# A hybrid attention and feed-forward layer on one core: ScalarE takes the forget logits, diagonal maxima in one masked pass, layer norm without a mean pass, and W1's first pieces on attention's tiles

## The chip, the cores and the metric

The kernel runs on one core of a Trainium2 chip. The metric is the device time of one execution in microseconds. TensorE (PE) does the matmuls and the transposes, VectorE (DVE), ScalarE (ACT) and GpSimd (POOL) the elementwise work, and SyncE (SP) and ScalarE's queue issue the transfers between HBM and the on-chip memory.

## The reference

One layer of a decoder, for a sequence of S = 2048 rows of width 1024, in float32:

```python
a = rms_norm(h, pre_mix_g)
z = a @ w_in                      # q | k | v (512 each) | forget logits (8) | u | v_sg (512 each)
y_att = forgetting_attention(q, k, v, f + f_bias)
y_sg = gelu(u) * (causal_mix(layer_norm(gelu(v_sg))) + bias)   # in chunks of 128 rows
y = concat(rms_norm(y_att), rms_norm(y_sg))
h = h + rms_norm(y @ w_out)
h = h + rms_norm(square(relu(rms_norm(h) @ w_ff1)) @ w_ff2)    # inner width 4096
h = h + sigmoid(h @ w_g + b_g) * (p @ w_pe)
```

Attention has 8 heads of 64. Its logits are q.k/8 + c[t] - c[s], where c is the running sum of log sigmoid(f + f_bias) over the rows, masked to s <= t. The layer norm takes a row's mean and its variance over 512 values, with a gain and an offset per column.

## The kernel before, in words

Every large matmul is done in three passes on operands split into a rounded part and the remainder (`mm3`, lines 102 to 106): high by high, high by low, low by high. The rounded parts are made by ScalarE or POOL, the remainders by VectorE or POOL (`split`, `halves_of`, `evac_split`).

**First stage (lines 221 to 523).** Four blocks of 512 rows. For each block, `block` runs six column groups of W_in, in the order v_sg's larger part (344 columns), the rest of u and v_sg (344), forget logits and u (344), q, k, v (512 each); each group has four output tiles n, and each output tile eight steps over the contraction. Step i = 4 x group + n names a place in this order, at which hooks hang other work: the layer norm from i = 8 on, `log_sigmoid` at 11, the running sum at 14, the spatial mix from 14 on, the next block's x at 11 to 22. Output tiles lie in two PSUM banks (`pacc`); the group's done function empties the bank. For the third group that is `fu_done` (lines 356 to 358): VectorE adds the bias to the 8 logits, then ScalarE applies gelu to the 336 columns of u in the same bank. For the second group it is `uv_done` (347 to 354): two gelus with row sums, the negative mean mu, `gv + mu` by VectorE (352), a Square with row sum by ScalarE. `layer_norm` (409 to 418) then takes the inverse deviation r and does (gv * r) * lng and + lnb on VectorE.

W_in's columns for the next group are loaded, rounded by ScalarE (line 96) and completed by POOL (line 100) in twelve tiles `wsp`, while the group before runs.

While block b is projected, a filler runs `maxima(b - 1)` (lines 142 to 189): the largest logit of each row over all keys, for each head, which attention's exponent needs. For a head and a key block c, four matmuls (one per 128 rows) write logits into the banks `pM` (two, and a third in this stage). VectorE reduces a bank to one column of `mx`. On the diagonal (c == b) it reduces the columns ahead of the last 128 and then handles the last 128 by a second operation that adds the triangular mask `dmask` and takes the maximum.

`log_sigmoid` (374 to 393) computes, for 512 rows and 8 heads held as 128 x 32, log sigmoid through a polynomial of eight terms, as a chain of small VectorE operations with one Sigmoid on ScalarE; `run_sum` (395) turns it into the running sum with two matmuls, one by the triangle `upper`, one by a tile of ones.

**Attention (528 to 930).** Heads and key blocks in an order written out by hand; the maxima of the last block and the projection by W_out of finished blocks run beside it.

**The passage (939 to 1256).** The projection of the last 512 rows (`last_proj`) runs with `prep_first` as filler, which normalises and transposes h for the feed-forward: `turn` goes through three tiles `px` and stores to `cS`, `join_now` makes the first two of four contraction steps of the operands B. The feed-forward's W1 product is done by seven products (a Strassen scheme) for each unit of 256 columns; `left` makes the sum of W1's blocks that a product needs, in two tiles `ws`, and splits it into one of three tiles `w1p`. The first unit runs in two halves: contraction steps 0 and 1 for all seven products, then 2 and 3, while `join` makes the operands of steps 2 and 3. `join` reads from `cS` into four tiles (`jraw`): the three px, and half of the tile w1raw[1]. `prep_next` does later what prep_first does, for the second half of the rows, with px as places too.

The order of instructions on each engine is set by the framework's scheduler, from the order in which the code traces them and from when it reckons them to be ready. Tiles live in pools that are stacked from two sides of the on-chip memory. A tile in a newly opened pool waits for the last use of those older tiles whose addresses it takes over. The three w1p lie in a pool of their own, `w1pp` (line 1134), opened after the projection's pools have been closed; its first tile takes over the addresses of the projection's last tiles, the two `z2` (lines 745 to 751 work on them).

Of the kernel before, what the change touches and what calls it, by code (L numbers as in the profile page):

```python
# [9 lines left out]
F32 = mybir.dt.float32  # L10
F32R = mybir.dt.float32r
AF = mybir.ActivationFunctionType
# [22 lines left out]
def trunk(ctx, tc, x, p, w_in, f_bias, sg_ln_g, sg_ln_b, sg_w, sg_b, att_out_g, sg_out_g,  # L35
# [4 lines left out]
    def pool(stack, name, bufs=1, space=None, side="left"):  # L40
# [30 lines left out]
    c_all = const1.tile([P, NT, H], F32, name="c_all")  # L71
    c0_all = const1.tile([P, NB, H], F32, name="c0_all")
    dmask_r = const1.tile([P, P], F32R, name="dmask")
# [4 lines left out]
    ident_r = const1.tile([P, P], F32R, name="ident_r")  # L78
    ve.tensor_copy(ident_r, ident)

# [58 lines left out]
    for t in QM:  # L139
        ve.memset(t[HD:HD + 2].bitcast(F32), 1.0)  # L140

    def maxima(b):

# [13 lines left out]
        for h in range(H):  # L157
            q = QM[h % 2]
            sc.dma_start(q[:HD].bitcast(F32), qS[b, h, :HD])
            mx = msm.tile([P, 4, 6], F32, name="mx")  # L160
            po.memset(mx, NEG)
            for c in range(b + 1):
                km = KM[n % NKM]
                n += 1
                sc.dma_start(km[:HD + 2].bitcast(F32), kS[c, h, HD:])
                for tt in range(4):
                    w = TB if c < b else P * (tt + 1)
                    ps = place_m()
                    pe.matmul(ps[:, :w], q[:, tt * P:(tt + 1) * P], km[:, :w], start=True, stop=True)  # L169
                    full = w if c < b else w - P  # L170
                    if full:
                        ve.tensor_reduce(mx[:, tt, c:c + 1], ps[:, :full], AX.X, ALU.max)  # L172
                    if c == b:
                        dg = ps[:, w - P:w]
                        ve.tensor_tensor_reduce(out=dg, in0=dg, in1=dmask, scale=1.0, scalar=NEG,
                                                op0=ALU.add, op1=ALU.max, accum_out=mx[:, tt, 5:6])
# [44 lines left out]
    with ExitStack() as ph:  # L221
# [19 lines left out]
        sgb = cst.tile([P, H], F32, name="sgb")  # L241
        ones = cst.tile([P, P], F32, name="ones")
        upper = cst.tile([P, P], F32, name="upper")
# [3 lines left out]
        def prep_consts():  # L247
            sy.dma_start(fb, f_bias[0].partition_broadcast(P))
            sy.dma_start(g_sgo, sg_out_g[0].rearrange("(k p) -> p k", p=P))
            sy.dma_start(lng, sg_ln_g[0].partition_broadcast(P))  # L250
            sy.dma_start(lnb, sg_ln_b[0].partition_broadcast(P))
            sy.dma_start(sgb, sg_b[0].rearrange("g t -> t g"))
            ve.memset(csum[:, 0], 0.0)
            ve.memset(ones, 1.0)
            po.affine_select(out=upper, in_=ones, pattern=[[1, P]], compare_op=ALU.is_ge, fill=0.0,
                             base=0, channel_multiplier=-1)
# [71 lines left out]
        def block(b, aT, hooks, fill, first=None):  # L328
# [18 lines left out]
            def uv_done(tt, ps):  # L347
# [3 lines left out]
                ve.tensor_scalar(mu[:, tt:tt + 1], mu[:, tt:tt + 1], -1.0 / AW, None, ALU.mult)  # L351
                ve.tensor_scalar(gv[:, tt], gv[:, tt], mu[:, tt:tt + 1], None, ALU.add)
                junk = sg1.tile([P, 512], F32, name="junk")
                sc.activation(junk, gv[:, tt], AF.Square, accum_out=ss[:, tt:tt + 1])

            def fu_done(tt, ps):
                ve.tensor_tensor(zf[:, tt], ps[:, :H], fb, ALU.add)
                sc.activation(ug[:, tt, :336], ps[:, H:344], AF.Gelu_apprx_tanh)  # L358
# [15 lines left out]
            def log_sigmoid():  # L374

                ve.tensor_scalar(e, zf, -1.0, None, ALU.mult)
                ve.tensor_tensor(e, zf, e, ALU.min)
                sc.activation(e, e, AF.Sigmoid)
# [3 lines left out]
                ve.tensor_tensor(s2, s_, s_, ALU.mult)  # L382
                ve.tensor_scalar(pl, s2, 1.0 / 17, 1.0 / 15, ALU.mult, ALU.add)
                for k in (13, 11, 9, 7, 5, 3, 1):
                    ve.tensor_tensor(pl, pl, s2, ALU.mult)
                    ve.tensor_scalar(pl, pl, 1.0 / k, None, ALU.add)
                ve.scalar_tensor_tensor(pl, pl, -2.0, s_, ALU.mult, ALU.mult)
                ve.tensor_scalar(zf, zf, 0.0, None, ALU.min)
                ve.tensor_tensor(pl, pl, zf, ALU.add)
                ve.tensor_copy(car[:, 0], csum[:, b])  # L390
# [4 lines left out]
            def run_sum():  # L395
                ps = pmx.tile([P, 512], F32, name="pmx")
                pe.matmul(ps[:, :32], upper, pl.rearrange("p a h -> p (a h)"), start=True, stop=False)
                pe.matmul(ps[:, :32], ones, car[:, 0:4].rearrange("p a h -> p (a h)"), start=False, stop=True)
                ve.tensor_copy(c_all[:, 4 * b:4 * b + 4].rearrange("p a h -> p (a h)"), ps[:, :32])
# [9 lines left out]
            def layer_norm():  # L409

                r = rstd_of(small, ss, 4, AW, "lnr")
                for tt in range(4):
                    ve.scalar_tensor_tensor(gv[:, tt], gv[:, tt], r[:, tt:tt + 1], lng, ALU.mult, ALU.mult)
                    ve.tensor_tensor(gv[:, tt], gv[:, tt], lnb, ALU.add)
                    po.tensor_scalar(vn[:, 0, tt], gv[:, tt], 1.0, 0.0, ALU.mult, ALU.add)
# [547 lines left out]
    ws = [fsm.tile([P, 4, P], F32, name=f"ws{e}") for e in range(2)]  # L963
    px = [w1q.tile([P, 4, P], F32, name=f"px{e}") for e in range(3)]

# [7 lines left out]

    _, w1raw = w1_places(w1q)


# [103 lines left out]

    flat = [t.rearrange("p a b -> p (a b)") for t in px]

# [14 lines left out]
    def prep_next():  # L1097

        for k in (3, 2, 1, 0):
# [6 lines left out]

            yield from join_now(k, 1, place, done, flat[0], flat[1], px[2], px[2])

    raws, nraw, nleft = {}, 2, 0
    lefts = {}  # L1110
# [22 lines left out]
    mix_stack.close()  # L1133
    w1p = w1_pieces(pool(w1s, "w1pp", side="right"))

# [227 lines left out]
    for i, (u, n, ks) in enumerate(run):  # L1363
        if i == len(JR):
# [3 lines left out]
            ctc = pool(fl, "ctc")  # L1368
            hqp = pool(fl, "hqp")
            for t in ((0, 0), (0, 1), (1, 0), (1, 1), 5, 6):  # L1370
                hq[t] = hqp.tile([P, 512], F32, name="hq" + str(t).strip("()").replace(", ", "_"))
# [250 lines left out]
```

## Time and profile before

| | |
|---|---|
| median of three runs | 2703.38 us (2702.57 to 2706.26) |
| the profiled execution | 2701.87 us, with a span of 2700.1 us |
| clock granted to PE, mean over the span | 0.989 |
| busy share of the span | PE 97%, PEld 79%, DVE 68%, ACT 50%, POOL 30% |
| HBM traffic | 174 GB/s over the span |

The span runs from the first instruction to the last; times in the views count from its start. Matmuls overlap, and their ends are modelled, so PE's idle time is read from the waits rather than from the starts. In a row of a timeline, the bracket at the end says how long the engine stood idle before the instruction and which instruction of which engine released it. Lines are those of the kernel before; L104 to L106 are the three passes of mm3, wherever it is called.

### The profile page before, as it was taken

How to read it: one execution, taken by the hardware profiler on the slowest of the kernel's cores; microseconds unless marked ns; L12 is line 12 of the kernel's file. 1: busy time of each engine (PE TensorE's matmuls, PEld its weight loads, DVE VectorE, ACT ScalarE, POOL GpSimd, SP SyncE). 2: the span in 40 equal slices, each digit the busy share in tenths (PEclk: the TensorE clock that was granted, in tenths of full speed). 3: DMA queues.
4: the chain of work that ended last, by engine and by line, in shares of the span. 5: the costliest groups of instructions: out<-in, count | busy, mean ns of one | idle time of the engine just before them, and what ended most of it. 6: DMA issues, size and time to landing. Idle time of an engine off the chain costs nothing.

```text
span 2700.1 us, 37436 instructions
## 1 busy us (share of the span) xinstructions
PE 2613.7 (97%) x12316; PEld 2123.4 (79%) x12316; DVE 1841.5 (68%) x3212; ACT 1342.4 (50%) x2632; POOL 811.5 (30%) x695
## 2 busy tenths in 40 slices
PE   8999999999899999969999999999999999999999
PEld 7787978777677777757788788888888888888887
DVE  5547576866778655578888676668886596875443
ACT  6444433358777777555555554544445444453111
POOL 5444343510000000253444332325451171501211
PEclk9999999999999999989999999999999999999999
DMA  5565756598868766454665854447556654673331
GB/s 169 151 183 145 195 141 171 145 218 211 210 177 190 175 182 151 137 164 165 224 210 175 296 193 148 150 155 247 171 191 223 187 160 132 210 250 115 109 119 61
DMA packets 440611, 472.85 MB, mean 175 GB/s; under 512 B 155616, under 2 KB 269664, under 8 KB 440416
## 3 DMA queue, kind: packets, MB, share of 16 engines
q1 hardware_dynamic: 430179, 454.39, 57.0%
q10 hardware_dynamic: 10237, 16.07, 2.2%
q8 instruction: 97, 1.59, 0.3%
q14 instruction: 98, 0.80, 0.1%
HBM read 336.38 MB, written 133.96 MB: 174 GB/s over the span
## 4 chain that ended last, share of the span: by engine, by line
PE 53%; DMA 2%; DVE 1%; issue 1%; ACT 1%; POOL 0%; SPq 0%; DVEq 0%; ACTq 0%; POOLq 0%
PE pf L106 17%; PE pf L104 17%; PE pf L105 17%; PE pf L1470 1%; DMA w1raw<-in_w_ff_dram 0%; DMA px<-hS 0%; DMA cS<-px 0%; DVE w1p L994 0%; DMA B<-jS 0%; PE pf L1018 0%; DVE ws L1170 0%; DVE hq L1189 0%; DVE z L748 0%; POOL tmp L1068 0%; DMA ysT<-ysS 0%
## 5 line engine op out<-in xcount | busy, mean ns | idle before, releaser
L104 PE MATMUL pf<-B,w1p 128*128 128x512 f32 x752 | 298.3, 397 | 14.4 <-ACT w1p L991 13.6
L106 PE MATMUL pf<-B,w1p 128*128 128x512 f32 x752 | 296.1, 394 | 2.8 <-DVE w1p L994 2.7
L1197 POOL TENSOR_TENSOR hq<-hq,hq 128x512 f32<-128x512 f32 x128 | 197.0, 1550 | 335.4 <-ACT hq L1191 298.3
L105 PE MATMUL pf<-B,w1p 128*128 128x512 f32 x752 | 297.1, 395 | 0.0
L660 DVE TENSOR_TENSOR hl<-pr,hl 128x512 fp32r<-128x512 f32 (+1 forms) x320 | 191.9, 608 | 102.7 <-ACT hl L659 86.0
L100 POOL TENSOR_TENSOR wsp<-wraw,wsp 128x344 fp32r<-128x344 f32 (+1 forms) x176 | 200.1, 1154 | 192.0 <-ACT wsp L96 181.6
L651 ACT ACTIVATE pr<-pS,bias 128x512 f32<-128x512 f32 (+1 forms) x320 | 196.6, 623 | 106.1 <-PE pS L647 64.0
L172 DVE TENSOR_REDUCE mx<-pM 128x1 f32<-128x512 f32 (+3 forms) x288 | 169.8, 597 | 78.7 <-PE pM L169 78.0
L104 PEld LDWEIGHTS pf<-B,w1p 128*128 128x128 f32 x752 | 141.7, 188 | 48.9 <-ACT w1p L991 14.1
L104 PE MATMUL pacc<-wsp,wide 128*128 128x344 f32 (+1 forms) x480 | 166.7, 347 | 9.7 <-ACT ug L358 6.8
L104 PE MATMUL pf<-R,L 128*128 128x512 f32 x452 | 175.9, 389 | 0.0
L106 PE MATMUL pf<-R,L 128*128 128x512 f32 x452 | 175.8, 389 | 0.0
L105 PE MATMUL pf<-R,L 128*128 128x512 f32 x452 | 175.8, 389 | 0.0
L106 PEld LDWEIGHTS pf<-B,w1p 128*128 128x128 f32 x752 | 141.5, 188 | 37.5 <-DVE w1p L994 4.4
L105 PEld LDWEIGHTS pf<-B,w1p 128*128 128x128 f32 x752 | 141.7, 188 | 31.9
L106 PE MATMUL pacc<-wsp,wide 128*128 128x344 f32 (+1 forms) x480 | 162.7, 339 | 0.5 <-DVE wide L117 0.5
L105 PE MATMUL pacc<-wsp,wide 128*128 128x344 f32 (+1 forms) x480 | 162.4, 338 | 0.0
L659 ACT CAST hl<-pr 128x512 fp32r<-128x512 f32 (+3 forms) x272 | 146.6, 549 | 6.5 <-PE pO L674 0.8
L991 ACT CAST L<-lr 128x512 fp32r<-128x512 f32 x113 | 70.3, 622 | 149.6 <-PE pf L105 119.5
L994 DVE TENSOR_TENSOR L<-lr,L 128x512 fp32r<-128x512 f32 x113 | 96.1, 851 | 68.0 <-ACT L L991 67.7
L994 DVE TENSOR_TENSOR w1p<-ws,w1p 128x512 fp32r<-128x512 f32 (+1 forms) x136 | 117.4, 869 | 35.7 <-ACT w1p L991 33.8
L991 ACT CAST w1p<-w1raw 128x512 fp32r<-128x512 f32 (+1 forms) x123 | 73.4, 598 | 128.5 <-PE pf L105 124.2
(443 smaller groups left out, 7199.1 us busy)
## 6 DMA issues: line engine op xcount, KB each, us to landing
hidC<-hq SPq DMA_DIRECT2D x224, 256.0 KB
lr<-hidC SPq DMA_DIRECT2D x224, 256.0 KB
w1raw<-in_w_ff_dram SPq DMA_DIRECT2D x64, 512.0 KB
w1raw<-in_w_ff_dram SPq DMA_DIRECT2D x128, 256.0 KB
wraw<-in_w_in_dram SPq DMA_DIRECT2D x96, 256.0 KB
wraw<-in_w_in_dram SPq DMA_DIRECT2D x88, 172.0 KB
KM<-kS ACTq DMA_DIRECT2D x80, 132.0 KB
jS<-C SPq DMA_DIRECT2D x19, 512.0 KB
```

The lines of the kernel that those rows point to most:

```text
L100: e.tensor_tensor(dst[:, 1], src, dst[:, 0].bitcast(F32), ALU.subtract)
L104: pe.matmul(ps, l[0], r[0], start=first, stop=False)
L105: pe.matmul(ps, l[0], r[1], start=False, stop=False)
L106: pe.matmul(ps, l[1], r[0], start=False, stop=last)
L172: ve.tensor_reduce(mx[:, tt, c:c + 1], ps[:, :full], AX.X, ALU.max)
L651: sc.activation(pr[:, off:], ps[:, off:], AF.Exp, bias=bias_of(b)[:, j, h:h + 1])
L659: sc.copy(hl[:, 0, off:], pr[:, off:])
L660: ve.tensor_tensor(hl[:, 1, off:], pr[:, off:], hl[:, 0, off:].bitcast(F32), ALU.subtract)
L991: sc.copy(dst[:, 0], src)
L994: (po if lo == "pool" else ve).tensor_tensor(dst[:, 1], src, dst[:, 0].bitcast(F32), ALU.subtract)
L1197: po.tensor_tensor(t, x, y, op)
L1470: pe.transpose(ps[:, kk], hts[t][g][:, kk * P:(kk + 1) * P], ident)
```

## The change

- **Forget logits.** In `fu_done` ScalarE copies the 8 logits out of the bank; the bias is added by VectorE once per block, at the head of `log_sigmoid`, on 128 x 32.
- **log_sigmoid.** The sum of negation and minimum becomes one operation, each Horner step becomes one (it was two), and the last steps are joined: 17 VectorE operations instead of 24.
- **Layer norm.** `gv + mu` goes; the Square takes mu as its bias; `layer_norm` becomes (gv + mu) * lng, then (.) * r + lnb.
- **Diagonal maxima.** One operation over all columns of the bank, with a mask `wmask` of 512 columns (384 zeros, then the triangle), its last w columns used; mx has four columns instead of six.
- **Small moves.** `ident_r` is made ahead of `dmask`; the tile of ones goes, and a broadcast column of `upper` stands for it.
- **W1's pieces.** The three w1p are allotted in w1q, the pool that is opened when attention's pools have been closed and before the projection of the last rows. To make room, px keeps one tile of its own and has the two ws as the others; jraw becomes both halves of w1raw[1], v_t and the last px; prep_next gets two tiles `pxn` from a later pool.

```diff
             for c in range(b + 1):
...
-                    full = w if c < b else w - P
-                    if full:
-                        ve.tensor_reduce(mx[:, tt, c:c + 1], ps[:, :full], AX.X, ALU.max)
-                    if c == b:
-                        dg = ps[:, w - P:w]
-                        ve.tensor_tensor_reduce(out=dg, in0=dg, in1=dmask, scale=1.0, scalar=NEG,
-                                                op0=ALU.add, op1=ALU.max, accum_out=mx[:, tt, 5:6])
+                    if c < b:
+                        ve.tensor_reduce(mx[:, tt, c:c + 1], ps, AX.X, ALU.max)
+                    else:
+                        ve.tensor_tensor_reduce(out=ps[:, :w], in0=ps[:, :w], in1=wmask[:, TB - w:], scale=1.0, scalar=NEG,
+                                                op0=ALU.add, op1=ALU.max, accum_out=mx[:, tt, c:c + 1])
...
-                ve.tensor_scalar(gv[:, tt], gv[:, tt], mu[:, tt:tt + 1], None, ALU.add)
                 junk = sg1.tile([P, 512], F32, name="junk")
-                sc.activation(junk, gv[:, tt], AF.Square, accum_out=ss[:, tt:tt + 1])
+                sc.activation(junk, gv[:, tt], AF.Square, bias=mu[:, tt:tt + 1], accum_out=ss[:, tt:tt + 1])
...
-                ve.tensor_tensor(zf[:, tt], ps[:, :H], fb, ALU.add)
+                sc.copy(zf[:, tt], ps[:, :H])
                 sc.activation(ug[:, tt, :336], ps[:, H:344], AF.Gelu_apprx_tanh)
...
-                ve.tensor_scalar(e, zf, -1.0, None, ALU.mult)
-                ve.tensor_tensor(e, zf, e, ALU.min)
+                ve.tensor_tensor(zf, zf, fb.unsqueeze(1).broadcast_to([P, 4, H]), ALU.add)
+                ve.scalar_tensor_tensor(e, zf, -1.0, zf, ALU.mult, ALU.min)
...
-                for k in (13, 11, 9, 7, 5, 3, 1):
-                    ve.tensor_tensor(pl, pl, s2, ALU.mult)
-                    ve.tensor_scalar(pl, pl, 1.0 / k, None, ALU.add)
+                for k in (15, 13, 11, 9, 7, 5, 3):
+                    ve.scalar_tensor_tensor(pl, pl, 1.0 / k, s2, ALU.add, ALU.mult)
...
-                    ve.scalar_tensor_tensor(gv[:, tt], gv[:, tt], r[:, tt:tt + 1], lng, ALU.mult, ALU.mult)
-                    ve.tensor_tensor(gv[:, tt], gv[:, tt], lnb, ALU.add)
+                    ve.scalar_tensor_tensor(gv[:, tt], gv[:, tt], mu[:, tt:tt + 1], lng, ALU.add, ALU.mult)
+                    ve.scalar_tensor_tensor(gv[:, tt], gv[:, tt], r[:, tt:tt + 1], lnb, ALU.mult, ALU.add)
...
-    px = [w1q.tile([P, 4, P], F32, name=f"px{e}") for e in range(3)]
+    px = [*ws, w1q.tile([P, 4, P], F32, name="px")]
...
     _, w1raw = w1_places(w1q)
+    w1p = w1_pieces(w1q)
...
-    jraw = [flat[e] for e in range(3)] + [w1raw[1].rearrange("p k f -> p (k f)")[:, :512]]
+    w1raw1 = w1raw[1].rearrange("p k f -> p (k f)")
+    jraw = [w1raw1[:, :512], w1raw1[:, 512:], v_t, px[2].rearrange("p a b -> p (a b)")]
...
-    w1p = w1_pieces(pool(w1s, "w1pp", side="right"))
```

More of the change, by code (lines that the diff above doesn't have):

```diff
@@ L72, in trunk @@
     c0_all = const1.tile([P, NB, H], F32, name="c0_all")
+    ident_r = const1.tile([P, P], F32R, name="ident_r")
+    ve.tensor_copy(ident_r, ident)
     dmask_r = const1.tile([P, P], F32R, name="dmask")
@@ L140, in trunk @@
         ve.memset(t[HD:HD + 2].bitcast(F32), 1.0)
+    wmask = mst.tile([P, TB], F32, name="wmask")
+    ve.memset(wmask[:, :TB - P], 0.0)
+    ve.tensor_copy(wmask[:, TB - P:], dmask)
     def maxima(b):
@@ L159, in maxima @@
             sc.dma_start(q[:HD].bitcast(F32), qS[b, h, :HD])
-            mx = msm.tile([P, 4, 6], F32, name="mx")
+            mx = msm.tile([P, 4, NB], F32, name="mx")
             po.memset(mx, NEG)
@@ L241, in trunk @@
         sgb = cst.tile([P, H], F32, name="sgb")
-        ones = cst.tile([P, P], F32, name="ones")
         upper = cst.tile([P, P], F32, name="upper")
@@ L253, in prep_consts @@
             ve.memset(csum[:, 0], 0.0)
-            ve.memset(ones, 1.0)
-            po.affine_select(out=upper, in_=ones, pattern=[[1, P]], compare_op=ALU.is_ge, fill=0.0,
+            ve.memset(upper, 1.0)
+            po.affine_select(out=upper, in_=upper, pattern=[[1, P]], compare_op=ALU.is_ge, fill=0.0,
                              base=0, channel_multiplier=-1)
@@ L382, in log_sigmoid @@
                 ve.tensor_tensor(s2, s_, s_, ALU.mult)
-                ve.tensor_scalar(pl, s2, 1.0 / 17, 1.0 / 15, ALU.mult, ALU.add)
-                for k in (13, 11, 9, 7, 5, 3, 1):
-                    ve.tensor_tensor(pl, pl, s2, ALU.mult)
-                    ve.tensor_scalar(pl, pl, 1.0 / k, None, ALU.add)
-                ve.scalar_tensor_tensor(pl, pl, -2.0, s_, ALU.mult, ALU.mult)
+                ve.tensor_scalar(pl, s2, 1.0 / 17, None, ALU.mult)
+                for k in (15, 13, 11, 9, 7, 5, 3):
+                    ve.scalar_tensor_tensor(pl, pl, 1.0 / k, s2, ALU.add, ALU.mult)
+                ve.scalar_tensor_tensor(pl, pl, 1.0, s_, ALU.add, ALU.mult)
                 ve.tensor_scalar(zf, zf, 0.0, None, ALU.min)
-                ve.tensor_tensor(pl, pl, zf, ALU.add)
+                ve.scalar_tensor_tensor(pl, pl, -2.0, zf, ALU.mult, ALU.add)
                 ve.tensor_copy(car[:, 0], csum[:, b])
@@ L397, in run_sum @@
                 pe.matmul(ps[:, :32], upper, pl.rearrange("p a h -> p (a h)"), start=True, stop=False)
-                pe.matmul(ps[:, :32], ones, car[:, 0:4].rearrange("p a h -> p (a h)"), start=False, stop=True)
+                pe.matmul(ps[:, :32], upper[:, P - 1:P].broadcast_to([P, P]), car[:, 0:4].rearrange("p a h -> p (a h)"), start=False, stop=True)
                 ve.tensor_copy(c_all[:, 4 * b:4 * b + 4].rearrange("p a h -> p (a h)"), ps[:, :32])
@@ L1079, in join_now @@
             yield
-    flat = [t.rearrange("p a b -> p (a b)") for t in px]
     def prep_first():
@@ L1105, in done @@
                     sy.dma_start(jS[m - 1, k - 1], place(m).bitcast(F32))
-            yield from join_now(k, 1, place, done, flat[0], flat[1], px[2], px[2])
+            yield from join_now(k, 1, place, done, *pxn, px[2], px[2])
+    pxn = None
     raws, nraw, nleft = {}, 2, 0
@@ L1369, in trunk @@
             hqp = pool(fl, "hqp")
+            pxn = [hqp.tile([P, 512], F32, name=f"pxn{e}") for e in range(2)]
             for t in ((0, 0), (0, 1), (1, 0), (1, 1), 5, 6):
```

2 lines of the change are left out of this document (removed).

## The prediction

> **What bounds the kernel now.** I read the page first, then the table of windows (67 us each), then who PE waited for in the first stage, then the timelines around the longest of those waits. A row of the windows gives, for a stretch, the busy us of PE, PEld, DVE, ACT and POOL with their instructions, the clock granted to PE, and the DMA engines' share and GB/s.
>
> ```profile
> span 2700.1 us, 37436 instructions
> ...
> PE 2613.7 (97%) x12316; PEld 2123.4 (79%) x12316; DVE 1841.5 (68%) x3212; ACT 1342.4 (50%) x2632; POOL 811.5 (30%) x695
> ```
>
> ```profile
> 1139.00:1206.00 67.00, 46.10 (x216) 37.22 (x215) 49.21 (x81) 35.29 (x81) 34.49 (x32) 0.86 0.61 193
> ...
> 2479.00:2546.00 67.00, 67.00 (x320) 55.60 (x319) 29.46 (x41) 12.49 (x24) 13.09 (x9) 1.00 0.38 120
> ```
>
> PE is busy for 2613.7 of 2700.1 us, so all that any edit off PE can win is the 86 us in which PE stands still, and the time that PE spends at half clock because it stood still. In the last third there is none of either (67.00 of 67.00 at clock 1.00); the worst window is the passage from the mixer to the feed-forward (46.10 of 67.00, clock 0.86). The edits of this change lie in two places: the first stage, and that passage. Nothing in it takes a matmul away, so each place is worth its idle time and its cold clock.
>
> What PE waited for in the first 670 us (total us, times, longest):
>
> ```profile
> PE pacc L104 <- ACT ug L358: 9.0, 5, 2.5
> PE pM L169 <- DVE mx L172: 5.0, 8, 1.3
> PE pacc L104 <- DVE stg L117: 4.0, 3, 1.9
> ...
> PE pacc L106 <- POOL wsp L100: 1.5, 3, 0.9
> ...
> PE pM L169 <- DVE lpl L385: 1.2, 1, 1.2
> ...
> PE pacc L104 <- ACT wsp L96: 0.9, 1, 0.9
> ...
> PE pacc L104 <- ACT gv L349: 0.7, 1, 0.7
> ```
>
> The largest entry names ACT, but ACT is not what is late. VectorE's and ScalarE's timelines show it:
>
> ```profile
> 57.04 3.45 DVE L413 SCALAR_TENSOR_TENSOR gv<-gv,lnr,lng 128x512 f32<-128x512 f32 x2 [1.13 <-POOL lnr L111]
> 60.41 0.15 DVE L357 TENSOR_TENSOR zf<-pacc,fb 128x8 f32<-128x8 f32 x1
> ```
>
> ```profile
> 60.60 0.45 ACT L358 ACTIVATE ug<-pacc 128x336 f32<-128x336 f32 x1 [2.59 <-DVE zf L357]
> ```
>
> ```profile
> 214.27 0.45 ACT L358 ACTIVATE ug<-pacc 128x336 f32<-128x336 f32 x1 [6.34 <-DVE zf L357]
> ```
>
> The forget logits (zf, 8 columns) and the gate's u (336 columns) sit in one PSUM bank, zf is read first, and by VectorE, whose queue holds two layer-norm operations of 3.45 us ahead of a 0.15 us add. ScalarE stands behind it, and with it the release of the bank. At 214 it stood 6.34 us, and the W_in casts queued behind it were then late for PE: the 1.5 and 0.9 us of wsp above.
>
> **The change part by part.** *Forget logits.* The add of L357 becomes a ScalarE copy; the bias is added once per block. ug then waits for PE alone. What stays is a bank emptied by ScalarE only, which is what L349 does: 0.7 us in all. So 9.0 - 0.7 = 8.3 us go. Cold clock follows those stalls:
>
> ```profile
> 74.00:78.00 4.00, 4.00 (x12) 3.18 (x11) 3.86 (x5) 1.58 (x3) 4.00 (x4) 0.57 0.24 72
> 204.00:208.00 4.00, 4.00 (x18) 4.00 (x17) 3.62 (x14) 2.25 (x5) 1.64 (x4) 0.61 0.22 67
> 218.00:222.00 4.00, 4.00 (x13) 3.15 (x12) 3.81 (x6) 1.58 (x4) 3.63 (x3) 0.65 0.60 145
> 1190.40:1204.00 13.60, 0.01 (x1) 0.00 (x0) 13.16 (x19) 7.72 (x18) 7.40 (x7) 0.62 0.50 165
> 1204.00:1208.00 4.00, 3.96 (x11) 3.12 (x12) 4.00 (x11) 1.93 (x6) 4.00 (x1) 0.59 0.00 0
> 1208.00:1224.80 16.80, 16.80 (x75) 13.69 (x74) 9.41 (x20) 6.26 (x13) 3.48 (x1) 1.00 0.16 46
> ```
>
> The first three stretches have a busy PE at clocks of 0.57, 0.61 and 0.65: 4 us x 0.43, 0.39 and 0.35 are 1.7, 1.6 and 1.4 us lost. The first two follow ug waits of at most 2.5 us: 3.3 us go with them. The third follows the wsp waits; they hang on the 6.34 us wait, so 2.4 us of idle and 1.4 us of clock are at stake, and I take 2.5 of the 3.8, since those casts also wait for their loads. On this the Trainium skill ("TensorE: Matmul & The Clock Gate", Part 1) says that the clock falls to half after an idle window of about 3.4 us; by it stalls of 2.5 us would leave the clock alone, and 3.3 + 1.4 us of my terms would not be theirs to give back. The rows above disagree with it, and it is a rival below.
>
> What the copy costs ScalarE, and the bias in the Square of the layer norm:
>
> ```profile
> L148 ACT COPY mr<-pM 8x128 f32<-8x128 f32 x24 | 5.9, 247 | 21.2 <-PE pM L146 17.6 <-DMA QM<-qS 3.6
> ```
>
> ```profile
> L116 ACT ACTIVATE stg<-pacc 128x512 fp32r<-128x512 f32 x44 | 26.2, 596 | 110.4 <-PE pacc L106 93.0 <-DMA qS<-stg 9.7 <-DMA wraw<-in_w_in_dram 3.3
> ...
> L116 ACT ACTIVATE wide<-tp,g_pre 128x512 fp32r<-128x512 f32 x24 | 16.5, 686 | 0.6 <-PE tp L301 0.6
> ```
>
> Sixteen copies at no more than 247 ns are 4.0 us, and a per-partition operand costs 686 - 596 = 90 ns, 1.4 us in sixteen Squares. ScalarE waits 93.0 us for pacc in the same stage, so 5.4 us hide there; if the cover were gone it would be those 5.4 us, and I charge 1.0. [...] Against the add's 0.15 us that is 16 x 0.1 = 1.6 us more engine time; here the queue in front of the engine, not the instruction, sets the price.
>
> *VectorE's other edits.*
>
> ```profile
> L175 DVE CUSTOM_DVE_ANT_0 pM<-pM,dmask 128x128 f32<-128x128 f32 x96 | 28.3, 297 | 9.8 <-PE pM L169 8.1
> ...
> L175 DVE DVE_READ_ACCUMULATOR2_ANT mx<- 128x1 f32 x96 | 13.5, 140 | 0.0
> ...
> L172 DVE TENSOR_REDUCE mx<-pM 128x1 f32<-128x384 f32 x24 | 13.2, 551 | 8.5 <-PE pM L169 8.4
> ...
> L352 DVE TENSOR_SCALAR gv<-gv,mu 128x512 f32<-128x512 f32 x16 | 10.2, 637 | 0.5
> L172 DVE TENSOR_REDUCE mx<-pM 128x1 f32<-128x256 f32 x24 | 10.1, 420 | 12.5 <-PE pM L169 12.5
> ...
> L386 DVE TENSOR_SCALAR lpl<-lpl 128x32 f32<-128x32 f32 x28 | 7.8, 278 | 0.5
> ...
> L172 DVE TENSOR_REDUCE mx<-pM 128x1 f32<-128x128 f32 x24 | 6.9, 287 | 13.9 <-PE pM L169 13.9
> ...
> L286 DVE CUSTOM_DVE_ANT_0 gv<-xt 128x512 f32<-128x512 f32 x2 | 1.4, 691 | 0.8 <-DMA xt<-in_x_dram 0.8
> ```
>
> Diagonal maxima: a head's four tiles now take 551 + 420 + 287 + 4 x (297 + 140) = 3.0 us. After it they are four passes of 128, 256, 384 and 512 columns; between the 297 of the 128-wide pass and the 691 of the 512-wide one (L286, the same operation) these are 297, 428, 560 and 691, with the read-outs 2.5 us. That is 0.5 us off each of 24 groups, 11 us of VectorE, of which PE sees something only where it waits for mx: of 5.0 us I take 0.5. Layer norm: 16 x 637 ns = 10.2 us go; of the two operations that stay the second becomes one of the first's kind. log_sigmoid: seven small operations of 24 go per block, 28 x 278 ns = 7.8 us. PE felt that chain directly (1.2 us at L385), and behind it VectorE's half of an evacuation, stg, was late by 4.0 us in all; the timeline shows one of these:
>
> ```profile
> 364.83 1.24 DVE L386 TENSOR_SCALAR lpl<-lpl 128x32 f32<-128x32 f32 x1
> ...
> 366.21 0.68 DVE L117 SCALAR_TENSOR_TENSOR stg<-pacc,stg 128x512 fp32r<-128x512 f32 x1
> ```
>
> The Horner part of the chain becomes half as long, which gives about half of 5.2 us: 2.5. The sum of the logits now waits for ScalarE's copies, with the filler's reductions behind it on VectorE; copies are done a block's group earlier than the sum is due, so I put that at nothing, and at 0.5 us a block if not. The other moves at the start (identity before mask, one tile less, a mask of 512 columns) are some half microsecond of VectorE while it waits for x. The first stage gives 8.3 + 3.3 + 2.5 + 0.5 + 2.5 - 1.0 = 16.1 us, between 6 (half of the logits' waits move on to the next wait) and 25 (all of stg, mx and wsp).
>
> *W1's rounded pieces.* The passage:
>
> ```profile
> 1204.04 0.79 PE L104 MATMUL pf<-B,w1p 128*128 128x512 f32 x1 [13.63 <-ACT w1p L991]
> ```
>
> ```profile
> 1199.98 0.93 SPq L749 DMA_DIRECT2D hS<-z  x2
> ```
>
> ```profile
> 1203.59 0.40 ACT L991 CAST w1p<-w1raw 128x256 fp32r<-128x256 f32 x1
> ```
>
> PE's last projection matmul ends at 1190.4 (1204.04 - 13.63); the first of the feed-forward needs a piece of W1 that ScalarE rounds at 1203.59. The pool w1pp is opened after the projection's pools close and lies over their last tiles, so the first piece waits until z is stored (issued 1199.98). In the new place, w1q, it lies over tiles of attention, which no later step reads. So the 13.6 us wait falls, and with it the cold stretch of 1204 to 1208 (4 x 0.41 = 1.6 us): 15.2 us is the upper end. The lower end is VectorE: in the gap it is busy 13.16 of 13.60 us, with the operands of the second half of the first unit. From 1190.4 until 1224.8, when that unit ends, it does 13.16 + 4.00 + 9.41 = 26.6 us of work. None of it vanishes; if none is done earlier, the unit can't end before 1190.4 + 26.6 = 1217.0, a gain of 7.8. PE alone would need 86 matmuls x 16.80/75 = 19.3 us, to 1209.7, a gain of 15.1. Some of the rounding will be done ahead, and some of the 9.41 is output work that PE doesn't need, but the gap's VectorE is full: I take 10.5. Px on ws, and join's inputs on other tiles, change which transfers the sums of W1 wait for (the stores of the last transposed blocks); PE's projection of the last 128 rows covers them. I put them at nothing, and, if that cover is gone, at one store as the trace has it: 3.6 us from 1199.98 to the cast that waited for it.
>
> Sum: 2701.87 - 16.1 - 10.5 = 2675.3 in the profiled execution's own terms. That execution (span 2700.1) is 1.5 us below the median of the three runs, 2703.38; from the median it is 2676.8.
>
> **Rivals.** *The stalls move on.* PE, no longer held by the logits, meets the next late thing (weights, maxima), and VectorE holds the first unit to the lower end: about 4 + 7.8 = 11.8 us, 2691.6. For it: VectorE's 97% in the gap, and wsp waits that are there already. Against it: those wsp waits come from the same 6.34 us. *The early place isn't used.* The casts of w1p may stay in ScalarE's queue behind the tail of the projection, where they are now: then only the 16.1 us are won, 2687.3. Against it: nothing but the tile ties them to z. *The clock falls for another reason* than these short stalls: then 3.3 + 1.4 us of it stay, 2681.5. For it: five ug waits, and a cold stretch behind only two. Against it: those two come straight after such waits. The rule of the Trainium skill above says the same as this rival. *Slower: the mask costs the shared port.* The 512-wide pass reads its mask from SBUF while POOL works. Operations with both inputs in SBUF pay for that: L413 took 3.45 us for two, 1.7 each, against 691 for L286. At 1.7/0.69 = 2.5 times, the four passes (1.98 us without their read-outs) cost 1.98 x 2.5 + 0.56 = 5.5 us a head instead of 3.0, 2.5 us more in each of 32 heads and blocks (8 of them in attention), 80 us of VectorE; with half of it seen by PE, through its two or three pM banks, 40 us against the gain of 26.6: 2717. It decides from a 512-wide pass of some 1.4 us on, where half of the extra time reaches 26.6 us. Against it: L175 has a mask in SBUF already and takes 297 ns, close to the plain reduction of 128 (287).
>
> **How the numbers follow.** The forecast has 0.57, with 2664 to 2687 as its own range (25 + 15.1 us; 6 + 10.5 us). The stalls moving on have 0.19, the unused place 0.12, the clock 0.05, the mask 0.07. The range for 8 in 10 reaches from 2664 over the first two rivals to 2694. A measurement of this kernel tells about 0.2%, 5.4 us, from no change: faster by more than that are the first four cases less a few that fall short, 0.88; the same 0.06; slower 0.06.
>
> **What would show it.** Right: in the new profile ug no longer waits for zf, PE's wait for ug falls under 1 us, no stretch near 74 and 204 below clock 0.9; 512-wide masked passes near 0.7 us; PE's wait for w1p of 13.6 us is under 4, and the first feed-forward matmul comes within a few us of the last projection one, with short waits for w1p or B after it, where VectorE is full. Wrong: as much idle time of PE in the first 600 us as before under other names, masked passes over 1.4 us, or w1p's first cast still just behind z's store.

## The result, and the profile after

The changed kernel took 2691.16 us (median of 8 runs, 2685.85 to 2698.36) beside 2703.47 us (8 runs, 2701.20 to 2712.84) for the kernel before on the same chip: a ratio of 0.9947 (95% interval 0.9932 to 0.9962). In terms of the 2703.4 us before, that is 14.3 us faster (10.3 to 18.4), where 26.6 had been forecast (2676.8). The profiled execution took 2691.64 us, with a span of 2689.8 us.

The page of the changed kernel first: PE has as much to do as before, VectorE 16.5 us less.

```profile
span 2689.8 us, 37253 instructions
...
PE 2612.5 (97%) x12316; PEld 2122.0 (79%) x12316; DVE 1825.0 (68%) x3058; ACT 1342.3 (50%) x2648; POOL 805.5 (30%) x695
```

**The passage** did what was forecast. The row of the table of windows that held 46.10 us of PE at a clock of 0.86 now reads:

```profile
1139.00:1206.00 67.00, 58.29 (x274) 47.25 (x273) 54.47 (x91) 39.38 (x90) 36.44 (x34) 0.96 0.63 200
```

PE's waits between 1170 and 1230 us in the changed kernel (total us, times, longest):

```profile
PE pf L105 <- DVE B L994: 2.7, 1, 2.7
PE pf L106 <- DVE w1p L994: 1.2, 3, 0.4
...
PE pf L104 <- ACT w1p L991: 0.6, 1, 0.6
```

The wait of 13.63 us for the first piece of W1 is gone: the first matmul of the feed-forward runs at 1179.1, between two of the projection, and the 0.6 us for ScalarE's rounding stand at 1218.8, behind the first unit. What is late now is VectorE: a remainder of B, for 2.7 us. The table of windows over the new passage, from the last projection matmul (1190.6) to the end of the first unit (1215.2), with its cold stretch:

```profile
1203.50:1206.90 3.40, 3.40 (x10) 2.64 (x9) 3.40 (x7) 1.20 (x2) 3.40 (x1) 0.50 0.00 0
...
1190.60:1215.20 24.60, 21.43 (x85) 16.84 (x84) 22.78 (x40) 13.31 (x30) 11.51 (x6) 0.93 0.30 97
```

Before, the same stretch ran from 1190.4 to 1224.8, 34.4 us; it is 24.6 us now. VectorE is busy for 22.78 of these.

**The first stage** gave much less than forecast. ug is gone from PE's waits, and their sum is what it was. The view for the changed kernel, from 30 to 556 us:

```profile
PE pacc L106 <- POOL wsp L100: 6.6, 6, 3.9
PE pacc L104 <- DVE stg L117: 6.0, 3, 3.1
PE pM L173 <- DVE mx L175: 5.3, 5, 1.6
PE tp L439 <- DVE gv L434: 3.3, 2, 2.3
...
PE pacc L104 <- ACT wsp L96: 1.3, 2, 0.9
...
```

With the six other rows, 5.3 us together, this is 27.8 us. The same view of the kernel before, added up in the same way, is 27.7 us. wsp by POOL went from 1.5 to 6.6 us, stg from 4.0 to 6.0, while the 9.0 us of ug went to nothing. In the profiled executions the last projection matmul of the first stage starts at 565.0 us before and 564.1 after, so this pair of traces shows 1 us of gain there. A trace can't say it more exactly: in the experiments below the first stage of the kernel before has a second trace, in which that matmul starts at 567.0 us, and the changed first stage has two, with 562.9 and 561.8 us and sums of waits of 23.9 and 27.8 us.

### The profile page after: what moved, and what is told of

The parts are those of the page before. It is cut to its first block, busy times and chain, and to the rows that moved or that the text cites. A ratio compares the mean times of both kernels' runs of the same rounds, so it can differ in the third digit from the quotient of the medians.

```text
span 2689.8 us, 37253 instructions
## 1 busy us (share of the span) xinstructions
PE 2612.5 (97%) x12316; PEld 2122.0 (79%) x12316; DVE 1825.0 (68%) x3058; ACT 1342.3 (50%) x2648; POOL 805.5 (30%) x695
## 4 chain that ended last, share of the span: by engine, by line
PE 54%; DVE 2%; DMA 1%; issue 1%; ACT 0%; POOL 0%; DVEq 0%; ACTq 0%; POOLq 0%; SPq 0%
PE pf L106 17%; PE pf L105 17%; PE pf L104 17%; DMA w1raw<-in_w_ff_dram 1%; PE pf L1471 1%; DVE ws L1170 0%; DVE w1p L994 0%; PE pf L1018 0%; DMA B<-jS 0%; DVE z L747 0%; DMA v<-hS 0%; DVE B L994 0%; PE pf L1464 0%; DMA hS<-z 0%; POOL tmp L1068 0%
## 5 line engine op out<-in xcount | busy, mean ns | idle before, releaser
L175 DVE TENSOR_REDUCE mx<-pM 128x1 f32<-128x512 f32 x192 | 129.8, 686 | 41.7 <-PE pM L173 41.1
L96 ACT CAST wsp<-wraw 128x344 fp32r<-128x344 f32 (+1 forms) x176 | 94.6, 549 | 100.9 <-DMA wraw<-in_w_in_dram 75.1
L173 PE MATMUL pM<-KM,QM 128*128 128x512 f32 (+2 forms) x320 | 119.5, 378 | 18.3 <-DMA KM<-kS 5.9
```

What stands on the lines that cost most here:

```text
L96: sc.copy(dst[:, 0], src)
L175: ve.tensor_reduce(mx[:, tt, c:c + 1], ps, AX.X, ALU.max)
```

## The experiments

The theory at first (A): the logits' copy frees the bank, PE runs ahead, and meets the remainders of W_in (wsp), which POOL makes in order behind other work that itself waits for VectorE. The rivals: (B) VectorE's sum of work sets the pace, whatever is moved; (E) waits only change their names. The kernels ran in three groups, each beside the kernel before on the same chip. Its median was 2703.97 us in the first (w1_only, first_only, zf_only, after_xn1), 2702.05 in the second (zf_xn1, before_xn1, xn1_vn, mask_only) and 2699.98 in the third (join_twice, ln_log_only, no_copy, split_log), so kernels of different groups are compared by their ratios to it. "Us" behind a ratio are its distance from 1 times 2703.4.

**The change in parts.** W1's pieces alone, with the new places of px, jraw and pxn (all of the diff from px on, applied to the kernel before):

```diff
-    w1p = w1_pieces(pool(w1s, "w1pp", side="right"))
+    w1p = w1_pieces(w1q)
```

> The kernel before with W1's pieces allotted in attention's place and nothing of the first stage's edits. Theory A (the passage gives what it was forecast to give, and the first stage gives next to nothing because PE, freed from the gate's wait, stands still for weights, evacuations and maxima instead): about 10 us less than before, 2693, ratio 0.9962, and PE's idle time before the first feed-forward matmuls under 4 us where it was 13.6. Rival B (the two halves share the gain): 5 to 7 us less, 2697, and the rest then is in the first stage alone.

Measured: 2691.50 us, ratio 0.9958 (0.9944 to 0.9972): 11.4 us (7.6 to 15.1). Everything in the first stage stayed, ug's 9.1 us too, and the passage shows the waits of the changed kernel:

```profile
PE pf L105 <- DVE B L995: 2.7, 1, 2.7
PE pf L106 <- DVE w1p L995: 2.1, 2, 1.6
```

The complement, the changed kernel with W1's pieces put back (the same lines the other way round):

> The changed kernel with W1's pieces put back behind the projection's tiles: the first stage's edits alone. Theory A: the wait for ug is gone, waits for wsp, stg and mx have grown by as much; the last projection matmul of the first stage within 2 us of the kernel before, and the whole 0 to 3 us less, 2701, ratio 0.999. Rival B: 5 us or more less, ratio 0.998 or under.

Measured: 2697.62 us, ratio 0.9979 (0.9969 to 0.9990): 5.7 us (2.7 to 8.4) for all of the first stage's edits, which had been given 16.1. That is more than theory A's 0 to 3 us and agrees with rival B's 5 or more, though the interval reaches into both; the first stage as a whole did gain something.

**The logits alone**, on the kernel before:

```diff
-                ve.tensor_tensor(zf[:, tt], ps[:, :H], fb, ALU.add)
+                sc.copy(zf[:, tt], ps[:, :H])
...
+                ve.tensor_tensor(zf, zf, fb.unsqueeze(1).broadcast_to([P, 4, H]), ALU.add)
```

> The kernel before with the forget logits' move to ScalarE alone (copy there, the bias added once a block). Theory A: PE's 9.0 us for ug go to under 1, wsp and stg take over 4 us or more of it, and the time falls by 0 to 4 us, 2701. The forecast's own step: 9.0 us of waits and 3 to 5 us of cold clock gone, 2692, ratio 0.996. Rival C (the masked pass and the layer norm in the change spoil what the logits win): zf alone is clearly faster than the first stage's edits together, 2695 or less.

Measured: 2704.11 us, ratio 1.0004 (0.9994 to 1.0013). The edit that carried 14 of the 26.6 us by itself is worth nothing that can be measured. PE's waits from 0 to 570 us show why:

```profile
PE pacc L106 <- POOL wsp L100: 8.3, 5, 4.7
PE pM L169 <- DVE mx L172: 7.5, 7, 2.5
```

In the first block it can be watched. PE's and POOL's timelines before, where PE stood 2.17 us for ug ahead of its first q tile, and then found its weights ready:

```profile
72.94 0.50 PE L104 MATMUL pacc<-wide,wsp 128*128 128x512 f32 x1 [2.17 <-ACT ug L358]
...
87.69 0.50 PE L104 MATMUL pacc<-wide,wsp 128*128 128x512 f32 x1 [1.72 <-DVE stg L117]
```

```profile
69.32 1.38 POOL L111 TENSOR_TENSOR xr<-xr,mhalf 128x1 f32<-128x1 f32 x2
70.36 1.42 POOL L100 TENSOR_TENSOR wsp<-wraw,wsp 128x512 fp32r<-128x512 f32 x1
73.27 1.38 POOL L111 TENSOR_TENSOR xr<-xr,mhalf 128x1 f32<-128x1 f32 x2 [1.49 <-DVE xr L110]
74.31 4.42 POOL L100 TENSOR_TENSOR wsp<-wraw,wsp 128x512 fp32r<-128x512 f32 x3
```

POOL's and PE's timelines of the kernel with only the logits' copy:

```profile
68.81 1.37 POOL L111 TENSOR_TENSOR xr<-xr,mhalf 128x1 f32<-128x1 f32 x2
71.62 1.37 POOL L111 TENSOR_TENSOR xr<-xr,mhalf 128x1 f32<-128x1 f32 x2 [1.44 <-DVE xr L110]
72.66 4.33 POOL L100 TENSOR_TENSOR wsp<-wraw,wsp 128x512 fp32r<-128x512 f32 x3
```

```profile
66.02 0.39 PE L104 MATMUL pacc<-wide,wsp 128*128 128x512 f32 x1
...
74.13 0.50 PE L106 MATMUL pacc<-wide,wsp 128*128 128x512 f32 x1 [4.68 <-POOL wsp L100]
...
87.71 0.50 PE L104 MATMUL pacc<-wide,wsp 128*128 128x512 f32 x1 [1.60 <-DVE stg L117]
```

The powers xr of the next block's normalisation are 0.7 us each, but they need results of VectorE (the second pair waits 1.44 us for one), and the remainders of W_in stand behind them. Before, one remainder stood between the two pairs; with the copy the scheduler put both pairs ahead of it. PE reaches its first q tile 6.9 us earlier (66.02 instead of 72.94) and waits 4.68 us for the first remainder, made at 72.66 instead of 70.36. The rest of the 6.9 us is a second short wait for wsp (0.52 us) and the clock, which is cold for 6.8 us from 74.2 on (0.54 over these) where it was for 3.4 us before: 1.7 us more. Then PE comes to the next wait, the one for VectorE's half of an evacuation (stg), which stands behind `log_sigmoid`; it leaves this wait at 87.71 us, where it left it at 87.69 before. Nothing is left of the gain.

**POOL's queue made shorter.** The next block's x normalised in one call, so one power per block instead of four, first on the changed kernel:

```diff
-                for tt in range(4):
-                    hooks[XN[tt]].append(lambda tt=tt: x_norm(box, ((tt, tt + 1),)))
+                hooks[XN[3]].append(lambda: x_norm(box, ((0, 4),)))
```

> The changed kernel, but the next block's x is normalised in one go (one power on POOL for four row tiles) in place of four, so that POOL has one wait for VectorE ahead of the weights' remainders instead of four. Theory A says that the weights' remainders in POOL's queue, behind these powers, are what PE meets: waits for wsp on PE fall from 6.6 + 1.3 us to under 3, and the time by 3 to 6 us against the changed kernel, 2687. If the loads of W_in or the weights' buffers hold them instead, wsp stays at 6 us or more and the time within 2 us of the changed kernel.

Measured: 2686.87 us, ratio 0.9937 (0.9923 to 0.9951). The interval overlaps that of the changed kernel (0.9932 to 0.9962), so it is not shown to be faster. Its waits for wsp by POOL are 4.0 us with none over 0.7, but those for wsp by ScalarE grew from 1.3 to 2.6 us, so that the sum is 6.6 where under 3 had been expected. The first attention scores start at 560.1 instead of 565.6 us:

```profile
PE pacc L106 <- POOL wsp L100: 4.0, 7, 0.7
```

The time, if not the waits, looked like theory A. Its test was the same edit on the kernel with the logits' copy, and on the kernel before:

> The kernel before with two edits: ScalarE copies the forget logits (the bias added once per block), and the next block's x is normalised in one call (one POOL power per block instead of four). Theory A (POOL runs in order, and the powers that wait for VectorE hold back the remainders of W_in, so that these were late behind the logits): with both edits the gain that the copy alone did not bring appears, 2694 to 2699 us, with PE's waits for wsp by POOL at 2 to 5 us instead of 8.3 and no wait for ug. Rival B (the stall is conserved whatever stands in POOL's queue, because VectorE's sum of work sets the pace): 2702 to 2706 us, the wsp waits replaced by waits for mx and stg of the same sum. Rival C (the single call is worth the same with and without the copy): the same gain as that call alone on the kernel before.

> The kernel before with only the single call for the next block's x. Theory A: the logits still hold their bank behind VectorE's layer norm, so ug's waits of 9 us stay and little is won: 2701 to 2704 us, ratio 0.999 to 1.000. Rival C: the call is worth its 4 us by itself, 2698 to 2700 us.

Measured: 2704.33 us, ratio 1.0012 (1.0001 to 1.0023), and 2702.54 us, ratio 1.0002 (0.9992 to 1.0012). Theory A in this form has fallen: with one power per block the copy's gain doesn't appear. PE's waits with both edits:

```profile
PE pacc L106 <- POOL wsp L100: 7.7, 8, 2.4
PE pM L169 <- DVE mx L172: 5.2, 7, 1.8
```

and POOL's timeline of the same kernel in the first block:

```profile
62.54 1.73 POOL L100 TENSOR_TENSOR wsp<-wraw,wsp 128x512 fp32r<-128x512 f32 x1
...
67.98 0.62 POOL L416 TENSOR_SCALAR vn<-gv 128x512 fp32r<-128x512 f32 x1 [1.41 <-DVE xss L293]
69.48 1.02 POOL L111 TENSOR_TENSOR xr<-xr,mhalf 128x4 f32<-128x4 f32 x1 [0.89 <-DVE xr L110]
70.47 4.62 POOL L100 TENSOR_TENSOR wsp<-wraw,wsp 128x512 fp32r<-128x512 f32 x3
```

Between 64.3 and 70.5 us no remainder of W_in is made: POOL stands in the layer norm's roundings (vn), and the power comes on top. The bracket of the second row names xss, the next block's sums of squares; what the rounding reads is gv, and VectorE writes that just before:

```profile
67.21 0.69 DVE L415 TENSOR_TENSOR gv<-gv,lnb 128x512 f32<-128x512 f32 x1
67.81 0.16 DVE L293 TENSOR_TENSOR xss<-xss 128x4 f32<-128x4 f32 x1
```

So the layer norm on VectorE, which held PE through zf and ug, can hold it through vn and wsp as well. Behind it stands the wait for stg: PE has only short waits for wsp here (2.41 us and three of 0.72), then waits 4.17 us for stg, and leaves that wait at 87.11 us. This form of the theory says that the roundings have to leave POOL.

```diff
-                    po.tensor_scalar(vn[:, 0, tt], gv[:, tt], 1.0, 0.0, ALU.mult, ALU.add)
+                    sc.copy(vn[:, 0, tt], gv[:, tt])
```

> The changed kernel with the single call and with the layer norm's rounding (vn, 16 operations of 0.6 to 1.1 us) on ScalarE instead of POOL. Theory A, extended (POOL's work beside VectorE is what is late now: it slows VectorE's two-input operations and delays wsp): another 2 to 4 us, 2683 to 2685 us, the layer norm's second operation and the subtraction under 0.9 us on the mean. Rival (ScalarE's casts of W_in are as tight as POOL): no change or 1 to 3 us slower than 2686.9, with waits for wsp by ScalarE over 3 us.

Measured: 2679.91 us in 6 runs (2678.00 to 2693.98), ratio 0.9930 (0.9911 to 0.9948). The view of PE's waits from 30 to 556 us:

```profile
PE pacc L104 <- DVE stg L117: 7.6, 2, 4.5
PE pM L173 <- DVE mx L175: 5.3, 8, 2.3
PE pacc L104 <- ACT ug L358: 3.4, 3, 1.8
...
PE pacc L106 <- POOL wsp L100: 0.2, 1, 0.2
```

With four rows of 4.7 us together the sum is 21.2 us instead of 27.8, wsp is 0.2, and the first scores start at 557.2 us. ug is back with 3.4 us: ScalarE now has vn ahead of it, which waits for VectorE. This is the lowest median of all kernels here, but its interval overlaps those of the changed kernel and of the single call, so it is not shown to be faster than either. VectorE's subtraction of the layer norm (L416), 1.22 us on the mean in the changed kernel, took 0.84 us here, as expected; the second operation (L413) did not come under 0.9 us but went from 1.14 to 1.34. In this kernel and the two made from it below, the last projection matmul of the first stage starts at 556.2 to 558.9 us in the traces, against 561.8 to 564.1 in the three traces of the changed first stage. A shorter first stage can be read there; by the ratios of all runs (0.9930, 0.9945 and 0.9947, beside 0.9947) a gain over the changed kernel isn't shown.

The same kernel with the logits taken back to VectorE's add:

```diff
-                sc.copy(zf[:, tt], ps[:, :H])
+                ve.tensor_tensor(zf[:, tt], ps[:, :H], fb, ALU.add)
...
-                ve.tensor_tensor(zf, zf, fb.unsqueeze(1).broadcast_to([P, 4, H]), ALU.add)
```

> The fastest version so far (single call for x, layer norm's rounding on ScalarE) with the logits taken back to VectorE's add. If the copy is worth something once the queues behind it are short: 4 to 9 us slower than that version's 2679.9, 2684 to 2689 us, with ug's waits above 6 us. If the copy was never worth anything (the layer norm's work, not the logits' place, is what counts): 2679 to 2682 us.

Measured: 2683.53 us, ratio 0.9945 (0.9933 to 0.9957), with 21.2 us of waits too, ug 4.3 of them. By the ratios this is 4.1 us slower than the version with the copy, with an interval from 2 us of gain to 10 of loss, and ug's waits didn't reach the 6 us of the first expectation. What the copy is worth when the other queues are short stays open.

**The masked pass alone**, on the kernel before (the diff's hunk on the maxima, the mask, and no tile of ones, to make room):

> The kernel before with only the single masked pass for the diagonal maxima (and the tile of ones left out, as in the change, to make room for the mask). The prediction's term: 0.5 us of gain in the first stage and nothing in attention, 2702 to 2703.5 us. Rival (the shorter VectorE queue is felt wherever PE waits for mx or stg, 9 us in all): 2698 to 2700 us. Rival on the other side (the mask read from SBUF beside POOL in attention, where the changed kernel's scores took 2 us longer): 2705 to 2707 us.

Measured: 2699.22 us, ratio 0.9981 (0.9970 to 0.9992): 5.1 us (2.2 to 8.1), the rival's amount and well above the term of 0.5; the two medians alone lie 2.8 us apart. The profiled execution is the slowest of its 11 runs, so its trace can't show where the gain lies, and that stays open. The longest of the passes in it, with what VectorE waited for ahead of it:

```profile
L177 DVE CUSTOM_DVE_ANT_0 pM<-pM,wmask 128x512 f32<-128x512 f32 x24 | 16.7, 695 | 10.4 <-PE pM L173 10.3
```

By now a theory D stood beside the others: what leaves VectorE's queue is felt in part, wherever it leaves it.

**Layer norm and log_sigmoid alone**, on the kernel before (their hunks of the diff, the logits still added by VectorE):

> The kernel before with only the layer norm without a mean pass and the shorter log_sigmoid (the logits still added by VectorE, the maxima in two passes). The prediction's terms for these: nothing for the layer norm and 2.5 us for the chain: 2699.5 to 2701.5 us. Theory D (every microsecond that leaves VectorE's queue between the second column group and the first q tile is felt about half, since PE's waits for ug, stg, mx and wsp are the same queue seen from several places; 18 us of operations leave): 2694 to 2698 us, with ug's waits under 6 us. Rival E (waits only change their names): 2701.5 to 2704 us.

Measured: 2702.37 us, ratio 1.0011 (0.9999 to 1.0024). VectorE's busy time between 30 and 556 us fell from 331.3 to 321.4 us and PE's waits rose from 27.7 to 29.3, ug's 9.9 among them, in a profiled execution that was the fastest of its 12 runs. Theory D has fallen in this form, and rival B with it: the sum of VectorE's work is not what PE feels. What PE meets is one place in VectorE's queue: in all fourteen traces it waits in the first block for stg, and leaves this wait between 84.1 and 88.0 us, 87.95 us here.

**The chain cut in three**, on the version with the lowest median:

```diff
                 ve.tensor_scalar(pl, s2, 1.0 / 17, None, ALU.mult)
+                yield
                 for k in (15, 13, 11, 9, 7, 5, 3):
                     ve.scalar_tensor_tensor(pl, pl, 1.0 / k, s2, ALU.add, ALU.mult)
+                yield
                 ve.scalar_tensor_tensor(pl, pl, 1.0, s_, ALU.add, ALU.mult)
...
+            lg = log_sigmoid()
+            for i in range(11, 14):
+                mine[i].append(lambda: next(lg, None))
```

> The fastest version so far with log_sigmoid's chain cut into three parts at three successive output tiles, so that VectorE's half of an evacuation (stg) can stand between the parts; the work is the same. Theory D (PE's 7.6 us of waits for stg are VectorE's queue behind that chain): these waits fall under 3 us and the time to 2674 to 2677 us. Rival E (the wait moves on to mx or wsp): 2679 to 2682 us with the sum of PE's waits in the first 566 us as before, some 26 us.

Measured: 2684.09 us, ratio 0.9947 (0.9931 to 0.9963), stg 8.0 us. VectorE's timeline of the first block shows that the edit didn't do what it was meant to:

```profile
81.61 2.49 DVE L386 SCALAR_TENSOR_TENSOR lpl<-lpl,lss 128x32 f32<-128x32 f32 x7
...
84.59 0.17 DVE L393 TENSOR_TENSOR car<-car,lpl 128x8 f32<-128x8 f32 x1
84.67 0.68 DVE L117 SCALAR_TENSOR_TENSOR stg<-pacc,stg 128x512 fp32r<-128x512 f32 x1
```

The scheduler put the three parts in a row again, ahead of stg. In the second and third block stg stands between two steps of the chain, but it does so without the cut as well. So the run decides nothing between theory D and rival E; that stg waits for this chain can be read, but that it would be worth its 7.6 us wasn't tried with success.

**The passage's new bound.** The changed kernel with seven remainders of B made twice:

```diff
+    halves = halves_of
...
+        def halves_of(dst, src, hi, lo):
+            halves(dst, src, hi, lo)
+            if k == 2:
+                ve.tensor_tensor(dst[:, 1], src, dst[:, 0].bitcast(F32), ALU.subtract)
```

> The changed kernel with the seven remainders of the third contraction step of B computed twice by VectorE (the second writes the same values): 7 x 0.68 = 4.8 us more VectorE work in the passage, nothing else. Theory A (the first unit of the feed-forward is now held by VectorE, as the prediction's lower end says): from the last projection matmul to the end of the first unit 28 to 30 us instead of 24.6, the whole 2694 to 2697 us. Rival (PE or the loads set it): within 1 us of the changed kernel in that stretch, 2690 to 2692 us.

Measured: the stretch from the last projection matmul to the end of the first unit took 26.1 us instead of 24.6, between the two expectations:

```profile
1190.80:1216.90 26.10, 22.52 (x86) 17.20 (x85) 24.52 (x43) 12.69 (x29) 14.32 (x7) 0.87 0.28 89
```

Three of the seven second remainders stand ahead of this stretch (at 1143.5, 1172.3 and 1179.4); the four in it are 2.7 us. Of these, 1.5 us were felt, and the clock of 0.87 instead of 0.93 is as much: 26.1 x 0.13 - 24.6 x 0.07 = 1.7 us. VectorE is nearly full there (busy for 24.52 of 26.10 us), but that it bounds the unit microsecond for microsecond is not shown. The whole took 2694.14 us, ratio 0.9983 (0.9973 to 0.9992); against the changed kernel's ratio that is more than 4.8 us can make. The changed kernel wasn't in that group, and what the rest is stays open.

## Why the prediction was half right

**W1's pieces: right.** 10.5 us forecast; 11.4 us (7.6 to 15.1) by the run with this part alone, and 34.4 - 24.6 = 9.8 us in the traces' stretch. The first unit ends at 1215.2, 1.8 us ahead of the 1217.0 that VectorE's work gave as the lower end, as VectorE does 22.8 us of work in the stretch instead of 26.6. Short waits for B (2.7 us) and w1p (0.4 us in the stretch) stayed, as forecast.

**The logits: wrong, and this is the step that failed.** The working took each of PE's waits for ug as time that comes back, 8.3 us, with 3.3 of clock and 2.5 of wsp behind them. ug did fall from 9.0 to nothing, and the copies took 0.15 us each, beside other work. But the alone run gave 1.1 us of loss (between 3.5 of loss and 1.6 of gain), and the sum of waits stayed at 27.5 us. The step that failed is this: that a wait of PE for ug, once removed, is time won, with nothing late behind it. With it fell the sentence that the late wsp hang on the 6.34 us wait: with ug's wait gone, those for wsp grew to 8.3 us. What stood behind, as the traces of the first block show it, were two more waits on the same VectorE: for wsp, whose maker POOL waits for the layer norm and the next block's normalisation, and then for stg, behind `log_sigmoid`. PE came 6.9 us earlier to the first and left the second at the same time as before. That the run without vn on POOL has 0.2 us of waits for wsp agrees with the first of these; no run took away the wait for stg, so the account is read from traces in part.

The rival "the stalls move on" had said this. That its 2691.6 is the measured time to half a microsecond is luck: its parts are 4 + 7.8, the two runs with one half each gave 5.7 and 11.4, and the forecast's own range, 2664 to 2687, was missed.

**The clock.** Its cold stretches were counted as gone with the waits. Between 30 and 556 us the kernel before has four, not the three of the prediction; the fourth begins at 367.6, behind a wait of 1.94 us for stg. After the change there are four again, one of them at 74 as before. The table of windows, the fourth of before and then those of the changed kernel:

```profile
367.60:371.00 3.40, 3.40 (x10) 2.61 (x9) 3.09 (x18) 0.26 (x1) 0.00 (x0) 0.50 0.78 219
```

```profile
73.70:77.10 3.40, 3.02 (x6) 1.62 (x6) 1.66 (x3) 1.95 (x3) 2.73 (x3) 0.50 0.67 184
87.30:90.70 3.40, 3.40 (x9) 2.65 (x9) 0.50 (x1) 0.00 (x0) 0.00 (x0) 0.50 0.81 230
213.60:217.00 3.40, 3.18 (x7) 2.08 (x8) 3.30 (x4) 1.77 (x4) 3.29 (x3) 0.50 0.40 118
548.10:551.50 3.40, 3.40 (x13) 2.92 (x13) 3.04 (x6) 0.69 (x1) 0.00 (x0) 0.50 0.30 66
```

and PE's waits ahead of these last four:

```profile
72.31 0.50 PE L106 MATMUL pacc<-wide,wsp 128*128 128x512 f32 x1 [3.88 <-POOL wsp L100]
...
86.31 0.50 PE L104 MATMUL pacc<-wide,wsp 128*128 128x512 f32 x1 [3.06 <-DVE stg L117]
...
213.69 0.79 PE L104 MATMUL pacc<-wide,wsp 128*128 128x512 f32 x1 [0.86 <-ACT wsp L96]
...
546.55 0.33 PE L439 MATMUL tp<-ident,gv 128*128 128x128 f32 x1 [2.25 <-DVE gv L434]
```

The Trainium skill ("TensorE: Matmul & The Clock Gate", Part 1) has the clock fall after an idle window of about 3.4 us; the first row agrees with it, the others came behind waits of 3.06, 0.86 (with three of 0.71 and less in the 5 us before) and 2.25 us.

Each cold stretch stands behind waits, so the step that tied the clock to short stalls can hold; but not every such wait brings one (2.09 us at 61.10 in the kernel before did not), and the same wait can bring one or not. The wait for stg of 1.72 us at 87.69 left the kernel before at full clock; in the run with W1's pieces alone, whose first stage is the same code, it was 1.87 us, and this followed:

```profile
87.70:91.10 3.40, 3.40 (x9) 2.63 (x10) 2.07 (x10) 0.60 (x1) 0.00 (x0) 0.51 0.76 201
```

So a cold stretch, 3.4 us at about half clock and thus 1.7 us, can't be booked to one wait as the terms of 3.3 and 1.4 us did. Whether the rival with another reason is right can't be told, since the waits did not go away.

**The maxima: right in the work, wrong in the worth.** The 512-wide pass takes 697 ns (691 forecast), a head's four with their read-outs (697 + 564 + 428 + 296 + 4 x 141) 2.55 us (2.5 forecast). The rival in which the mask costs the shared port is out. The term of 0.5 us was mis-sized: alone, the pass is worth 5.1 us (2.2 to 8.1), about as much as the whole first stage, and why is not shown.

**log_sigmoid and the layer norm:** 2.5 us forecast; alone, 3.0 us of loss (0.3 of gain to 6.5 of loss). The chain's Horner part did become shorter. In the run alone the wait for stg fell from 4.0 to 2.6 us, as the term said, but those for ug and mx rose to 9.9 and 6.8. In the changed kernel stg went to 6.0 us: in the first block PE, freed elsewhere, began to wait 2.7 us earlier than before (83.25 instead of 85.97) and was let go only 1.4 us earlier (86.31 instead of 87.69). The three parts and W1's add up to -11.4 + 1.1 - 5.1 + 3.0 = -12.4 us, beside 14.3 measured for all, so within the intervals the gain is W1's pieces and the masked pass. But the three parts alone come to 1.0 us and the first stage as a whole to 5.7 (2.7 to 8.4), so it isn't excluded that the parts are worth more together than each by itself.

**What would show it.** No wait for ug, passes near 0.7 us, no long wait for w1p: as written. That no stretch near 74 is cold was not: the clock was 0.50 from 73.7 to 77.1. The sign for wrong, as much idle time in the first 600 us under other names, was there as well.

## What to carry to other kernels

A wait is worth its length only if whatever is late behind it is not also late: before a stall is priced, ask when each other input of the waiting instruction, and of those right after it, would have been ready, and through which queues the same slow producer reaches them. An engine that runs in order passes its waits on to everything behind, so be wary of putting an operation that waits for VectorE on POOL ahead of weights that don't; taking it away brought the waits for those weights from 4.0 to 0.2 us here, though no gain clear of the spread. And run each suspected part alone on the chip before summing terms: the part with the largest term was worth nothing that could be measured, and one with a term of 0.5 us was worth 2 to 8.

## What the runs showed of the hardware

How long VectorE's smallest operations take depends on POOL. In the kernel before, one operation of the polynomial's chain in two of its repetitions, with POOL's instruction beside the first:

```profile
84.36 1.32 POOL L100 TENSOR_TENSOR wsp<-wraw,wsp 128x512 fp32r<-128x512 f32 x1 [0.77 <-ACT wsp L96]
```

```profile
84.56 1.15 DVE L386 TENSOR_SCALAR lpl<-lpl 128x32 f32<-128x32 f32 x1
...
85.97 0.18 DVE L386 TENSOR_SCALAR lpl<-lpl 128x32 f32<-128x32 f32 x1
```

The first starts while POOL's instruction runs and ends with it (at 85.71, POOL's at 85.68), after 1.15 us; the second starts behind it and takes 0.18 us. So a chain of small operations costs by the POOL instructions that it meets more than by its count. And runs of one kernel spread by 5 us and more to either side, and two traces of the same first stage end it 2 us apart (565.0 and 567.0): a single trace can name a wait of 2 us here, but not size it.
